# Layer 0's output projection: half of its contraction by Strassen's block products, two output tiles at a time

## The chip, the cores and the metric

The kernel runs on one core of a Trainium2 chip. The metric is the device time in microseconds (us) of one execution, as the median of several runs. The engines are named as in the profile: PE (TensorE matmul), PEld (its weight load), DVE (VectorE), ACT (ScalarE), POOL (GpSimd) and SP (SyncE, which only issues DMAs here).

## The reference, cut to what matters

One inference step of a two-layer decoder trunk over 576 tokens (512 prompt, 64 sample). Layer 0 is a short gated convolution, layer 1 an mLSTM block.

```python
def short_conv_mixer(h, buf, w_in, conv_w, w_out):
    b_gate, c_gate, xa, z = jnp.split(h @ w_in, 4, axis=-1)
    u = c_gate * xa
    conv, new_buf = causal_dwconv(u, buf, conv_w)
    y = b_gate * conv * jax.nn.silu(z)
    return y @ w_out, new_buf          # y: 576 x 2048, w_out: 2048 x 1024
...
x = x + out                            # residual, then layer 1
```

The change touches only `y @ w_out` of layer 0 and the addition to the residual.

## The kernel before, in words

Everything is kept transposed: a tile holds 128 features as partitions and the 576 tokens as columns. A product in float32 accuracy is made of three matmuls in a reduced format: each operand is split into a high part `hi` (an ACT cast) and a rest `lo` (a DVE subtraction), and `step` and `plain` issue weight-hi x data-hi, weight-hi x data-lo and weight-lo x data-hi. Each of these needs two matmuls, since 576 columns don't fit in one bank: `gemm` (L235) cuts them as 256 and 320 (`HALVES`), `plain` (L433) as 288 and 288 (`HT`).

Weights lie in HBM as chunks of 128 outputs x 1024 contraction rows, in the order in which they are used. A chunk is loaded by SP into one of four raw buffers (`wr`, 512 KB) and converted in halves of four 128x128 blocks: ACT cast `wh`, DVE subtraction `wl` (L215/L216 in `split_weights`, L264/L265 in `parts_of`), into four rotating buffers each.

Layer 0's input projections already use Strassen's scheme (in Winograd's form) in `block_pair`: two output tiles by two contraction tiles, the 576 columns cut in halves, seven products of 288 columns instead of eight. Its weight sums come from the blocks `a11, a12, a21, a22` of two raw chunks; in layer 0 (`layer0[0]` true) two of them are made by DMA: POOL issues accumulating loads (L312, L313), the others by DVE (L350, L354). Its data forms come from `forms(xa, xb)`: eight DVE operations (four of 288 columns in `mixed`, L271 to L274; three subtractions of 576 columns, L167; one of 288, L288) and four ACT operations, where a plain split of two tiles takes two DVE operations and two ACT casts. The seven products are issued by `product` (L345) into PSUM banks `p`; ACT copies some banks (L357, L362, L365, L375, L378), DVE adds the rest.

For each of 16 feature tiles f, layer 0 makes u, the convolution `cv` and the gate z, and multiplies them (L614 to L663). Block products for f+1's u and for f's z and b alternate on PE. The result is split at once into `ya` (hi, lo): L166, L167. Tiles of 576 columns come from one pool of 70 slots (`N_SLOT`), scratch of layer 0 from a second one with 7 slots (`X`).

Then comes the output projection, the loop over the 8 output tiles m:

```python
for m in range(KD):
    acc = gemm(64 + 2 * m, 2, ya)     # 2 chunks x 8 tiles x 3 x 2 = 96 matmuls
    x = T(name="x")
    load(out=x, in_=io["xT"][m])
    nc.vector.tensor_tensor(x, flat(acc), x, ALU.add)      # L678
```

followed by a store of x, its split for layer 1 (`h2`: L169, L170) and the sum of squares (L460 to L464). Layer 1 begins with `gemm(80, ...)` over `h2`.

The order of the instructions on each engine is not the order of the text: a planner gives each engine, when the program is built, the earliest instruction in the text whose operands and buffers it thinks ready. The queues then run in that fixed order, and an instruction that waits holds up those behind it on its engine; this holds for SP's and POOL's DMA issues too.

The functions that the change touches, and the part of the main function that calls them:

Of the kernel before, what the change touches and what calls it, by code (L numbers as in the profile page):

```python
# [12 lines left out]
ALU = mybir.AluOpType  # L13
# [6 lines left out]
KD = D // P  # L20
# [47 lines left out]
def trunk(tc, io):  # L68
    nc = tc.nc
    ctx = ExitStack()  # L70
    with ctx:
# [90 lines left out]
        def split(src, scale=None, n=NT):  # L162

            hi, lo = R(n, "hi"), R(n, "lo")
            if scale is None:
                nc.scalar.copy(hi, src)  # L166
                nc.vector.tensor_tensor(lo, src, hi.bitcast(F32), ALU.subtract)  # L167
            else:
                last_hi[:] = [nc.scalar.activation(hi, src, AF.Copy, scale=scale).ins]  # L169
                nc.vector.scalar_tensor_tensor(lo, src, scale, hi.bitcast(F32), ALU.mult, ALU.subtract)  # L170
            return hi, lo
# [151 lines left out]
            ahead_of[c1, c2] = groups, behind  # L323

        def block_pair(c1, c2, fs, xs, out1, out2, add, mid=None, then=None, pops=0, groups=None,
                       behind=()):

# [69 lines left out]
            if xs is None:  # L397
                tt(o22, p, m5, ALU.subtract)
# [26 lines left out]
        def plain(ba, bb, chunk, xs, start, w=()):  # L425

            w = w or weights(chunk)
            n = 4 * len(w)
            for k in range(n):
                (hi, lo), (xh, xl) = w[k // 4], xs[k]  # L430
                for i, (a, x) in enumerate(((hi, xh), (hi, xl), (lo, xh))):
                    for b, t in ((ba, 0), (bb, HT)):
                        nc.tensor.matmul(b, a[:, k % 4, :], x[:, t:t + HT], start=bool(start) and k == 0 and i == 0,  # L433
                                         stop=(k == n - 1 and i == 2), skip_group_check=True)
                if k % 2:
                    run()
                    if n == 8:
                        drip()

        def gemm_pair(c1, c2, fs, xs, out1, out2, mid=None, then=None, pops=0):  # L440


            if (c1, c2) not in ahead_of:
                block_weights(c1, c2)
            block_pair(c1, c2, fs, xs, out1, out2, False, mid, then, pops)
# [12 lines left out]
        def sumsq(ssq, x, first, eng=nc.vector):  # L458
            if first:
# [140 lines left out]
        nc.vector.tensor_tensor(rb2, rb, rb, ALU.mult)  # L600

        cpa = const.tile([P, NW, 2], F32, name="cpa")
        ya = []
        ext = None
        cx = raws[0:2]
        for f in range(NW):
# [54 lines left out]
            nc.scalar.activation(z, z, AF.Silu)  # L661
            nc.vector.tensor_tensor(cv, b_ if second else product(3), cv, ALU.mult)
            nc.vector.tensor_tensor(cv, cv, z, ALU.mult)  # L663
            ya.append(split(cv))
            if f % 4 == 3:
                store(out=io["exa_out"][f // 4], in_=ext)
        load_buffers("C", "states1", 2)
        layer0[0] = False
        store(out=io["cpa_out"], in_=cpa)

        x1s = dram.tile([KD, P, NT], F32, name="x1s")
        ssq = T(name="ssq")
        h2 = []
        for m in range(KD):
            acc = gemm(64 + 2 * m, 2, ya)
            x = T(name="x")
            load(out=x, in_=io["xT"][m])
            nc.vector.tensor_tensor(x, flat(acc), x, ALU.add)  # L678
# [945 lines left out]
def _arrays(a):  # L1624
# [6 lines left out]
    wts = np.concatenate([t.reshape(-1, P, KD, P) for t in (  # L1631
        ain, _chunks(f["a_w_out"][0]), bin_[:NW], _chunks(f["b_w_v"][0]), kq, bin_[NW:], _chunks(f["b_w_out"][0]))], 0)

    blk = [c for c in range(8, 64) if c % 4 < 2 or c // 4 in SECOND]
    wts[blk] = wts[blk][:, :, [0, 2, 4, 6, 1, 3, 5, 7]]
    cols = np.zeros((P, NCOL), np.float32)

# [81 lines left out]
```

## Time and profile before

| what | value |
|---|---|
| runs (3) | 1655.02, 1655.08 (median), 1656.1 us |
| span of the profiled execution | 1654.3 us (its time with what lies around the span isn't recorded apart) |
| PE busy | 1627.4 us, 98% of the span |
| DVE, ACT, POOL busy | 1125.8, 806.9, 148.8 us |
| granted TensorE clock, mean | 0.994 |

Layer 0's block products fill the span up to about 376 us, the output projection runs from there to about 489 us, layer 1 follows. A row of a window view gives, after the window's bounds and length, the busy time of PE, PEld, DVE, ACT and POOL with the instructions counted, then the granted clock (1.00 is full), the share of DMA and GB/s. A row of a timeline gives start, duration, engine, line, operation, output<-input, shape, and in brackets how long its engine sat idle before and what ended that. A group of instructions gives the count, the busy time, the mean ns of one, and the idle time before.

### The profile page before, as it was taken

To read this page: it belongs to the slowest core of one execution; us is meant where nothing else is said; L and a number is where in the kernel's file an instruction comes from. 1 tells how busy PE (TensorE), PEld (TensorE's weight loads), DVE (VectorE), ACT (ScalarE), POOL (GpSimd) and SP (SyncE) were. 2 spreads that over 40 slices of the span, in tenths; PEclk is the share of its full clock that TensorE was granted. 3 is DMA by queue.
4 is the path that set the end of the run, shared out by engine and by line. 5 is a ranking of instruction groups with operands and counts; after the bars stand their busy time and mean duration, and the time that the engine had idled before them with its cause. 6 is when DMAs were issued, how large, how long until landed. Compare 5 with 4: busy or idle time off the path is not lost. (4 is left out here: it accounts for less than half of the span.)

```text
span 1654.3 us, 31177 instructions
## 1 busy us (share of the span) xinstructions
PE 1627.4 (98%) x12029; PEld 1548.7 (94%) x12029; DVE 1125.8 (68%) x2124; ACT 806.9 (49%) x1622; POOL 148.8 (9%) x295
## 2 busy tenths in 40 slices
PE   9999999999999999999999999999999998999998
PEld 9999999999999999999899989899898787989997
DVE  7988898885337976555966456446458658688775
ACT  5566666653324553434645344344345456556431
POOL 1111111110001000000111010110101000000000
PEclk9999999999999999999999999999999899999999
DMA  6476666654332434535434554454556587998992
GB/s 219 111 174 167 175 168 159 175 136 148 120 120 91 149 121 128 172 119 159 156 103 151 156 177 162 142 188 140 173 190 241 186 280 262 336 341 296 359 342 103
DMA packets 121893, 301.61 MB, mean 182 GB/s; under 512 B 12656, under 2 KB 35056, under 8 KB 121744
## 3 DMA queue, kind: packets, MB, share of 16 engines
q1 hardware_dynamic: 98320, 267.61, 48.7%
q0 software_dynamic: 8064, 14.68, 5.8%
q10 hardware_dynamic: 15360, 17.32, 3.1%
q8 instruction: 94, 1.54, 0.4%
q14 instruction: 55, 0.45, 0.1%
HBM read 235.91 MB, written 63.66 MB: 181 GB/s over the span
## 5 line engine op out<-in xcount | busy, mean ns | idle before, releaser
L345 PE MATMUL p<-hi,wh 128*128 128x288 f32 x1540 | 454.4, 297 | 3.9 <-ACT p L357 1.9
L345 PE MATMUL p<-lo,wh 128*128 128x288 f32 x1540 | 452.6, 294 | 0.0
L345 PE MATMUL p<-hi,wl 128*128 128x288 f32 x1540 | 450.7, 295 | 0.2 <-DVE wl L265 0.2
L345 PEld LDWEIGHTS p<-hi,wh 128*128 128x128 f32 x1540 | 288.5, 188 | 12.7 <-DVE ws L350 4.1
L345 PEld LDWEIGHTS p<-lo,wh 128*128 128x128 f32 x1540 | 289.0, 188 | 0.0
L345 PEld LDWEIGHTS p<-hi,wl 128*128 128x128 f32 x1540 | 287.9, 188 | 0.4 <-DVE wl L265 0.4
L264 ACT CAST wh<-wr 128x512 fp32r<-128x512 f32 (+1 forms) x298 | 171.4, 578 | 215.4 <-PE p L345 123.5
L265 DVE TENSOR_TENSOR wl<-wr,wh 128x512 fp32r<-128x512 f32 (+1 forms) x298 | 185.0, 635 | 94.9 <-ACT wh L264 92.5
L235 PE MATMUL acc<-hi,wh 128*128 128x256 f32 (+1 forms) x1072 | 233.4, 298 | 1.8 <-ACT xm L711 1.0
L235 PE MATMUL acc<-lo,wh 128*128 128x256 f32 (+1 forms) x1072 | 231.9, 297 | 0.0
L235 PE MATMUL acc<-hi,wl 128*128 128x256 f32 (+1 forms) x1072 | 231.7, 297 | 0.0
L264 ACT CAST wh<-ws 128x512 fp32r<-128x512 f32 (+1 forms) x201 | 114.8, 573 | 203.8 <-PE p L345 129.6
L215 ACT CAST wh<-wr 128x512 fp32r<-128x512 f32 x170 | 104.7, 619 | 201.2 <-PE acc L235 148.1
L235 PEld LDWEIGHTS acc<-hi,wh 128*128 128x128 f32 x1072 | 180.4, 190 | 7.4 <-issue 1.6
L216 DVE TENSOR_TENSOR wl<-wr,wh 128x512 fp32r<-128x512 f32 x170 | 116.7, 689 | 98.7 <-ACT wh L215 88.6
L235 PEld LDWEIGHTS acc<-hi,wl 128*128 128x128 f32 x1072 | 179.9, 190 | 1.6 <-issue 1.3
L235 PEld LDWEIGHTS acc<-lo,wh 128*128 128x128 f32 x1072 | 179.9, 190 | 0.6 <-issue 0.2
L265 DVE TENSOR_TENSOR wl<-ws,wh 128x512 fp32r<-128x512 f32 (+1 forms) x201 | 125.5, 630 | 68.7 <-ACT wh L264 68.0
L1236 DVE SCALAR_TENSOR_TENSOR c<-c,cols,r 128x512 f32<-128x512 f32 x128 | 91.5, 743 | 27.0 <-PE r L1235 24.9
L433 PE MATMUL p<-hi,wh 128*128 128x288 f32 x496 | 109.2, 300 | 0.0
L433 PE MATMUL p<-hi,wl 128*128 128x288 f32 x496 | 107.3, 295 | 0.0
L433 PE MATMUL p<-lo,wh 128*128 128x288 f32 x496 | 107.0, 295 | 0.0
(388 smaller groups left out, 2619.1 us busy)
## 6 DMA issues: line engine op xcount, KB each, us to landing
wr<-wts SPq DMA_DIRECT2D x222, 512.0 KB, 3.6
c<-cs SPq DMA_DIRECT2D x112, 512.0 KB, 5.8
cs_out<-c SPq DMA_DIRECT2D x64, 512.0 KB, 7.5
ws<-wts SPq DMA_DIRECT2D x28, 256.0 KB, 4.5
ws<-wts POOLq DMA_DIRECT2D x28, 256.0 KB, 4.7
wr<-wts POOLq DMA_DIRECT2D x28, 256.0 KB, 4.1
x<-xcs SPq DMA_DIRECT2D x20, 288.0 KB, 4.8
x<-xT SPq DMA_DIRECT2D x16, 288.0 KB, 4.3
```

Source lines behind the costliest of these rows:

```text
L215: last_act[0] = nc.scalar.copy(hi, raw[:, 4 * i:4 * i + 4, :]).ins
L216: nc.vector.tensor_tensor(lo, raw[:, 4 * i:4 * i + 4, :], hi.bitcast(F32), ALU.subtract)
L235: nc.tensor.matmul(acc[:, o:o + j - i], a[:, k % 4, :], x[:, i:j], start=(first and k == 0 and p == 0), stop=(last and k == 7 and p == 2))
L264: last_act[0] = nc.scalar.copy(hi, src).ins
L265: nc.vector.tensor_tensor(lo, src, hi.bitcast(F32), ALU.subtract)
L345: nc.tensor.matmul(bank_, a[:, j, :], x, start=(start and n + j + i == 0), stop=(n == len(groups) - 1 and j == len(g) - 1 and i == 2), ski ...
L433: nc.tensor.matmul(b, a[:, k % 4, :], x[:, t:t + HT], start=bool(start) and k == 0 and i == 0, stop=(k == n - 1 and i == 2), skip_group_ch ...
L1236: ins = nc.vector.scalar_tensor_tensor(ct[:, j, :], ct[:, j, :], dec[:, o + j:o + j + 1], r, ALU.mult, ALU.add).ins
```

## The change

The contraction of 2048 is cut in two. Features 0 to 7 are multiplied as before, but by `plain` with equal halves; features 8 to 15 go through `block_pair`, for two output tiles (m, m+1) at a time, so four times. The tiles `ya[8:16]` are no longer split but kept as they are and made into `forms`: tiles 8 and 9 at f = 12, the other three pairs inside `gemm_first`, in the text behind the plain products of the first output pair. The first pair takes `gemm_first` (plain products first, then block products with the flag `add`), the other three take `gemm_pair` (block products first, then plain products into the same banks). With `onto`, the banks are added onto the residual rows, which are loaded ahead of the products. The store, the split and the sum of squares of two tiles follow each pair. Layer 0's scratch pool stays open until the projection is over, and the pool of the states opens there. On the host, the two chunks of each output tile change places and the blocks of one of them are reordered.

```diff
@@ block_pair(..., onto=False)
+            if onto:
+                tt(o12, o12, u, ALU.subtract)
+                plain(bx, bw, c1 + 1, xs, None)
+                tt(o11, bx, o11, ALU.add)
+                tt(o12, bw, o12, ALU.add)
+                tt(o22, o22, m5, ALU.subtract)
+                plain(by, bv, c2 + 1, xs, None)
+                tt(o21, by, o21, ALU.add)
+                tt(o22, bv, o22, ALU.add)
+                return
@@
-        def gemm_first(c1, c2, fs, xs, out1, out2, mid, then):
+        def gemm_first(c1, c2, fs, xs, out1, out2, mid, then, onto=False):
             mid = [go() for go in mid]
+            if onto:
+                block_weights(c1, c2)
             for c_, o in ((c1, out1), (c2, out2)):
                 ba, bb = block(), block()
                 plain(ba, bb, c_ + 1, xs, True)
-                nc.scalar.copy(o[:, 0:HT], ba)
-                nc.scalar.copy(o[:, HT:NT], bb)
-            work.extend([lambda: None, *mid])
-            block_pair(c1, c2, fs[0:4], None, out1, out2, True, then=then, pops=1)
+                for b, t in ((ba, 0), (bb, HT)):
+                    if onto:
+                        nc.vector.tensor_tensor(o[:, t:t + HT], b, o[:, t:t + HT], ALU.add)
+                    else:
+                        nc.scalar.copy(o[:, t:t + HT], b)
+            if onto:
+                for go in mid:
+                    go()
+            else:
+                work.extend([lambda: None, *mid])
+            block_pair(c1, c2, fs[0:4], None, out1, out2, True, then=then, pops=0 if onto else 1)
@@ layer 0, end of the loop over f
-            ya.append(split(cv))
+            ya.append(split(cv) if f < 8 else cv)
+            if f in (12,):
+                fy.append(forms(ya[8], ya[9]))
@@
-        load_buffers("C", "states1", 2)
-        layer0[0] = False
...
-        for m in range(KD):
-            acc = gemm(64 + 2 * m, 2, ya)
-            x = T(name="x")
-            load(out=x, in_=io["xT"][m])
-            nc.vector.tensor_tensor(x, flat(acc), x, ALU.add)
-            store(out=x1s[m], in_=x)
-            h2.append(split(x, col("norm1", m)))
-            sumsq(ssq, x, m == 0)
+        for m in range(0, KD, 2):
+            pair = [T(name="x") for _ in range(2)]
+            for i, x in enumerate(pair):
+                load(out=x, in_=io["xT"][m + i])
+            then = (68 + 2 * m, 70 + 2 * m) if m < KD - 2 else None
+            if m == 0:
+                more = [lambda j=j: lambda: fy.append(forms(ya[2 * j], ya[2 * j + 1])) for j in (5, 6, 7)]
+                gemm_first(64, 66, fy, ya[0:8], *pair, more, then, True)
+            else:
+                gemm_pair(64 + 2 * m, 66 + 2 * m, fy, ya[0:8], *pair, then=then, onto=True)
+            for i, x in enumerate(pair):
+                store(out=x1s[m + i], in_=x)
+                h2.append(split(x, col("norm1", m + i)))
+                sumsq(ssq, x, m + i == 0)
+        load_buffers("C", "states1", 2)
+        layer0[0] = False
@@ host
+    aout = _chunks(f["a_w_out"][0])[:, ::-1]
...
+    blk = [... as before ...] + list(range(64, 80, 2))
```

More of the change, by code (lines that the diff above doesn't have):

```diff
@@ L325, in block_pair @@
         def block_pair(c1, c2, fs, xs, out1, out2, add, mid=None, then=None, pops=0, groups=None,
-                       behind=()):
+                       behind=(), onto=False):
             if groups is None:
@@ L438, in plain, with gemm_pair @@
                         drip()
-        def gemm_pair(c1, c2, fs, xs, out1, out2, mid=None, then=None, pops=0):
+        def gemm_pair(c1, c2, fs, xs, out1, out2, mid=None, then=None, pops=0, onto=False):
             if (c1, c2) not in ahead_of:
                 block_weights(c1, c2)
-            block_pair(c1, c2, fs, xs, out1, out2, False, mid, then, pops)
-        def gemm_first(c1, c2, fs, xs, out1, out2, mid, then):
+            block_pair(c1, c2, fs, xs, out1, out2, False, mid, then, pops, onto=onto)
+        def gemm_first(c1, c2, fs, xs, out1, out2, mid, then, onto=False):
             mid = [go() for go in mid]
+            if onto:
+                block_weights(c1, c2)
             for c_, o in ((c1, out1), (c2, out2)):
@@ L602, in trunk @@
         cpa = const.tile([P, NW, 2], F32, name="cpa")
-        ya = []
+        ya, fy = [], []
         ext = None
@@ L1629, in _arrays @@
     bin_ = _chunks(f["b_w_in"][0])
+    aout = _chunks(f["a_w_out"][0])[:, ::-1]
     kq = np.stack([_chunks(f["b_w_k"][0]), _chunks(f["b_w_q"][0])], 1)
     wts = np.concatenate([t.reshape(-1, P, KD, P) for t in (
-        ain, _chunks(f["a_w_out"][0]), bin_[:NW], _chunks(f["b_w_v"][0]), kq, bin_[NW:], _chunks(f["b_w_out"][0]))], 0)
-    blk = [c for c in range(8, 64) if c % 4 < 2 or c // 4 in SECOND]
+        ain, aout, bin_[:NW], _chunks(f["b_w_v"][0]), kq, bin_[NW:], _chunks(f["b_w_out"][0]))], 0)
+    blk = [c for c in range(8, 64) if c % 4 < 2 or c // 4 in SECOND] + list(range(64, 80, 2))
     wts[blk] = wts[blk][:, :, [0, 2, 4, 6, 1, 3, 5, 7]]
```

## The prediction

> **What bounds the kernel now.** I read the page first, then a window view of the stretch in which the change lies and its neighbours.
>
> ```profile
> span 1654.3 us, 31177 instructions
> PE 1627.4 (98%) x12029; PEld 1548.7 (94%) x12029; DVE 1125.8 (68%) x2124; ACT 806.9 (49%) x1622; POOL 148.8 (9%) x295
> ...
> 300.00:340.00 40.00, 40.00 (x304) 40.00 (x304) 34.78 (x63) 25.16 (x53) 7.28 (x9) 1.00 0.68 171
> ...
> 360.00:390.00 30.00, 28.57 (x213) 28.10 (x213) 20.56 (x36) 14.24 (x28) 1.48 (x2) 1.00 0.45 135
> ...
> 404.00:482.00 78.00, 78.00 (x587) 78.00 (x587) 30.70 (x44) 23.56 (x37) 0.00 (x0) 1.00 0.40 132
> ```
>
> PE is the bound: busy 98% of the span, without a gap in the output projection (404 to 482) at clock 1.00, where DVE (30.7 of 78) and ACT (23.6) have much room. A matmul less there is time less. At the end of layer 0 it is different: DVE is busy 34.8 of 40 us before it, and across the transition (360 to 390) PE misses 1.43 us. Next, the timeline of DVE gives the rates and the waits:
>
> ```profile
> 118.61 0.45 DVE L398 TENSOR_TENSOR b<-pu,m 128x288 f32<-128x288 f32 x1
> ...
> 274.30 0.45 DVE L398 TENSOR_TENSOR b<-pu,m 128x288 f32<-128x288 f32 x1
> ...
> 365.79 0.69 DVE L354 TENSOR_TENSOR ws<-ws,wr 128x512 f32<-128x512 f32 x1 [1.53 <-DMA ws<-wts]
> ...
> 372.86 0.69 DVE L216 TENSOR_TENSOR wl<-wr,wh 128x512 fp32r<-128x512 f32 x1
> 373.46 0.75 DVE L167 TENSOR_TENSOR lo<-cv,hi 128x576 fp32r<-128x576 f32 x1
> 374.13 0.75 DVE L615 TENSOR_TENSOR u<-cx,cx 128x576 f32<-128x576 f32 x1
> ...
> 382.94 0.76 DVE L663 TENSOR_TENSOR cv<-cv,z 128x576 f32<-128x576 f32 x1
> ...
> 386.80 0.69 DVE L216 TENSOR_TENSOR wl<-wr,wh 128x512 fp32r<-128x512 f32 x1 [1.60 <-ACT wh L215]
> ...
> 389.61 0.76 DVE L678 TENSOR_TENSOR x<-acc,x 128x576 f32<-128x576 f32 x1 [2.12 <-PE acc L235]
> ...
> 479.21 0.76 DVE L678 TENSOR_TENSOR x<-acc,x 128x576 f32<-128x576 f32 x1 [2.08 <-PE acc L235]
> 480.81 0.82 DVE L170 SCALAR_TENSOR_TENSOR lo<-x,cols,hi 128x576 fp32r<-128x576 f32 x1 [0.25 <-ACT hi L169]
> ```
>
> The reader is to see three things. L678 ends each output tile: from 389.61 to 479.21 are seven tiles, so 12.80 us for 96 matmuls, 133.3 ns each. L398 of b ends a period of two block pairs (168 matmuls): seven periods from 118.61 to 274.30, 22.24 us each, 132.4 ns per matmul of 288 columns. And the last tile of layer 0 is ready only at 383.7 (L663), while u of that tile (L615) starts right behind the split that gives a slot back (L167).
>
> **Matmuls removed.** Before: 8 x 96 = 768 by 133.3 ns, 102.4 us. After, for each of four pairs: the plain half is 2 tiles x 8 x 3 x 2 = 96, the block half 7 products x 4 pairs of contraction tiles x 3 = 84, where plain needs 96. 4 x 180 = 720, all of 288 columns, by 132.4 ns: 95.3 us. The difference is 7.1 us: 6.4 from 48 matmuls and 0.7 from the equal halves. Nothing on PE hides this; it is the gain.
>
> The Trainium skill (TensorE: Matmul & The Clock Gate, Back-to-back issue gap) gives N/2.4 + 2.5 ns between warm matmuls, linear in the columns. By it 288 columns take 122.5 ns, equal halves gain nothing, and the saving would be an estimated 5.9 us; the row says 132.4, so the rule only fits within 8%, and I go by the row.
>
> **The transition, where the change adds work.** Ahead of the first block product stand two plain tiles, 96 x 132.4 ns = 12.7 us, which need only `ya[0:8]` and so start at the place of the old tile 0, to about 389.5. In that time three `forms` are to be made. How long one takes on DVE is seen in layer 1, together with what `gemm_first` costs there:
>
> ```profile
> 783.91 0.45 DVE L273 TENSOR_TENSOR fb<-x,x 128x288 f32<-128x288 f32 x1
> 784.28 0.45 DVE L274 TENSOR_TENSOR fb<-x,fa 128x288 f32<-128x288 f32 x1
> 784.64 0.69 DVE L216 TENSOR_TENSOR wl<-wr,wh 128x512 fp32r<-128x512 f32 x1
> 785.25 0.75 DVE L167 TENSOR_TENSOR lo<-fa,hi 128x576 fp32r<-128x576 f32 x1
> 785.92 0.75 DVE L167 TENSOR_TENSOR lo<-fb,hi 128x576 fp32r<-128x576 f32 x1
> 786.59 0.45 DVE L288 TENSOR_TENSOR hl<-x,hl 128x288 fp32r<-128x288 f32 x1
> 786.95 0.76 DVE L167 TENSOR_TENSOR lo<-x,hi 128x576 fp32r<-128x576 f32 x1
> ...
> L166 ACT CAST hi<-fa 128x576 fp32r<-128x576 f32 x14 | 9.4, 673 | 12.5 <-DVE fa L272 12.5
> ...
> PE p L345 <- ACT p L357: 1.9, 1, 1.9
> PE p L345 <- DVE hl L288: 0.7, 1, 0.7
> ...
> 800.00:815.00 15.00, 12.97 (x103) 11.45 (x102) 12.91 (x26) 10.21 (x23) 0.53 (x1) 1.00 0.38 116
> ```
>
> From start to start, 288 columns take 0.37 us, 576 take 0.67 and 512 take 0.60. A form is 5 x 0.37 + 3 x 0.67 = 3.9 us, three are 11.6. The ledger of DVE from 360 to 389.5 (29.5 us): 20.6 as before; less 1.3 (two splits), less 1.8 (seven halves of weights were converted there, L216 from 372.86 to 386.80; before the first block product only the four of chunks 65 and 67 are needed); plus 11.6; plus 2.4 (L354 and three L265 for the first products); plus 0.7 (two additions onto out1). That is 32.2 us. If u of the last tile is no longer held by a slot, its convolution (some 3 us from L615 on) moves ahead of 360 into DVE's gaps, and 29.1 are left. I expect that move: `ya[8:16]` as single tiles and one `forms` of 7 tiles hold about 68 of 70 slots at f = 15, some fewer than before. So PE would miss between 0 and 2.7 us, and the same function in layer 1 misses 2.03 (the window from 800 to 815, first for the last `hl`, then for the copy L357 that depends on the product so delayed). I take 2.0. ACT gets three casts of 0.67 us and a shorter copy per form, under 8 us in all, on top of 14.2 of 30, and is no bound.
>
> The wait of 1.43 us at 364 has another cause:
>
> ```profile
> 356.70 0.33 SPq L221 DMA_DIRECT2D wr<-wts  x1
> 357.07 0.42 SPq L311 DMA_DIRECT2D ws<-wts  x1
> ...
> SPq L221 <- DVE ws L350: 18.6, 2, 10.5
> ...
> 361.72 0.86 POOL L312 DMA_DIRECT2D ws<-wts  x1 [8.59 <-DMA ws<-wts]
> ```
>
> The load of chunk 64 waits on SP for a raw buffer until 356.70, and the load of a weight sum (L311) stands behind it; then POOL's accumulating load, then L354 at 365.79. In the new kernel two x loads and two block chunks come at this place and wait for the same buffer. I leave the 1.43 us in; its bounds are 0 and 1.43.
>
> **What moves or is added beside other work.** The forms of tiles 8 and 9 at f = 12: 3.9 us on DVE against 5 x 0.67 of splits that no longer come at f = 8 to 12; over one period of 22.2 us DVE (87% busy) would be full, and a weight conversion could be late by as much as about 1 us; I take 0, since conversions run two or three products ahead. Weights: 28 conversions of block weights take the place of 16 plain ones, 12 x 0.60 = 7.2 us more on DVE in 95 us, hidden under the 39% of that stretch. DMA: per pair a 256 KB load on SP and two accumulating ones on POOL more, at a DMA share of 0.40, with POOL idle there (0.00). The first plain weights (65, 67) come behind two block chunks on SP; before, the third and fourth loads were issued at 369.87 and 372.97 and
>
> ```profile
> 369.87 3.43 SPq L221 DMA_DIRECT2D wr<-wts  x2
> wr<-wts SPq DMA_DIRECT2D x222, 512.0 KB, 3.6
> ```
>
> land in 3.6 us: 65 is there at 373.5, converted by 375, needed at 376.6. That is covered by some 1.5 us; without that cover PE waits for the remainder. The additions onto x are six of 288 columns per pair instead of two of 576 (2.2 against 1.3 us start to start), under 11 us of other matmuls. The end: the last tile's additions, L169 and L170 end some 3 us after the last matmul (2 us before, from 479.2 to 481.6 at L170), and layer 1's first product needs that tile only for its last 6 of 48 matmuls, 5.6 us later; cost 0. The x loads now stand on SP ahead of their pair's weights, the stores behind the pair, as many as before; no engine waits for a store there.
>
> The three pairs of `gemm_pair` with `onto` have no row in this trace. Nearest is layer 1's `gemm_pair` with the same four raw buffers:
>
> ```profile
> L298 DVE TENSOR_TENSOR ws<-wr x39: 423/692/791, 552.3 to 1213.8; 128x512 f32<-128x512 f32 x24, 128x256 f32<-128x256 f32 x15
> ...
> 650.00:700.00 50.00, 50.00 (x384) 49.32 (x383) 29.92 (x53) 23.11 (x44) 3.62 (x8) 1.00 0.44 135
> ```
>
> The window has no idle time on PE: I take 0. Upper end: each waits once like f = 15 for its accumulated sum, 3 x 1.43 = 4.3 us. They have the plain half (12.7 us) as cover for a chain that took 8.7 us (357.07 to 365.79), so 0 is nearer. The first row shows when the states' pool is first written, at 552 us: that it now opens some 100 us later than before costs 0.
>
> **Sum.** -7.1 + 2.0 = -5.1 us. The span 1654.3 becomes 1649.2; the median of the runs, 1655.08, lies 0.8 above the span, so 1650.0.
>
> **Rivals.**
> A: nothing waits, and the 1.43 us go too, because the planner puts the sum's load ahead of the chunk on SP. For it speaks the ledger's lower end (29.1), against it that both `forms` and the last gate need DVE and ACT in turn. -8.5: 1646.6.
> B: the change doesn't deliver: the saving is handed back in waits, 32.2 us of ledger (2.7), hand-overs with ACT (1), and one wait per later half of the pairs (1 to 2). -7.1 + 5.5 = -1.6: 1653.5, no measurable change. DVE's 87% ahead of the transition speaks for it, the free 60% behind it against.
> C, slower: the planner keeps the forms in the text's order, behind the plain products' additions. Then DVE starts them at 389.5: 0.7 for the last additions, 11.6 for the forms, less the last 0.67, plus 0.67 for an ACT cast; only three quarters of the first two products (18 matmuls, 2.4 us) run meanwhile. PE misses 9.9 us. After 2.7 us without work in 4, the trace shows a lower clock:
>
> ```profile
> 1378.00:1382.00 4.00, 1.29 (x8) 1.06 (x8) 3.67 (x6) 3.71 (x12) 0.00 (x0) 0.94 0.54 148
> 1382.00:1386.00 4.00, 3.71 (x21) 3.31 (x20) 4.00 (x7) 2.23 (x5) 0.29 (x1) 0.64 0.71 249
> ```
>
> 0.36 of 4 us, 1.4 us more. -7.1 + 9.9 + 1.4 = +4.2: 1659.3. It is slower by 0.2% once the waits pass 10.4 us. Against it: L216 of chunk 64 (372.86) runs ahead of L615, which is earlier in the text, so DVE's order isn't the text's. The Trainium skill (TensorE: Matmul & The Clock Gate, Part 1) says an idle window of about 3.4 us halves the clock until about 3.4 us of work have passed; by that rule C would cost an estimated 1.7 instead of 1.4. The trace agrees: 1.00 after waits of 1.4 and 2.0 us, 0.64 after 2.7 in 4.
>
> **How the numbers follow.** The likeliest: 0.48. A 0.14, B 0.25, C 0.13. Measurement of this kernel tells 0.2%, 3.3 us. Faster (likeliest and A) 0.62, same (B) 0.25, slower (C) 0.13. The likeliest's own range is 1648 to 1652 (0 to 4 us of waits in the transition). The whole range reaches to A, 1646.5, and over B to 1655.5 (the three pairs waiting 4.3 and the transition 2.7, rounded up); C is left out.
>
> **What would show it.** Matmuls at L345 and L433 in the place of L235 between 376 and 482, and layer 1 starting 5 us earlier; PE idle behind `hl` or L357 near 389 of about 2 us (right), over 5 (B or C); the window of the later pairs with PE full; the forms' L271 of the last pairs before 389. Wrong it would be if PE waits for `wh` of the later pairs, or if the planner's new order opens gaps far behind, in layer 1.

## The result and the profile after

The changed kernel takes 1665.65 us (median of 4 runs, 1661.38 to 1666.48), the kernel before 1655.59 beside it; ratio 1.0053, interval 1.0039 to 1.0067. It is slower by more than the 0.2% that this kernel's measurement can tell, where 1650.0 had been forecast. The profiled execution is one of 1666.03 us.

The page after, and the window view of the stretch around the change (columns as before), first the kernel before over the whole stretch, then the changed one:

```profile
span 1664.2 us, 31238 instructions
PE 1626.0 (98%) x11981; PEld 1545.6 (93%) x11981; DVE 1150.2 (69%) x2188; ACT 823.9 (50%) x1658; POOL 156.4 (9%) x303
```
```profile
340.00:410.00 70.00, 68.57 (x514) 68.10 (x514) 46.56 (x77) 33.35 (x64) 3.80 (x5) 1.00 0.48 139
```
```profile
300.00:345.00 45.00, 44.40 (x335) 44.17 (x335) 41.50 (x77) 29.03 (x61) 8.56 (x11) 1.00 0.67 166
360.00:375.00 15.00, 13.53 (x101) 13.10 (x100) 9.06 (x17) 7.26 (x16) 2.33 (x3) 1.00 0.51 137
375.00:390.00 15.00, 14.30 (x105) 13.75 (x105) 12.16 (x23) 7.93 (x17) 0.87 (x1) 1.00 0.64 187
390.00:400.00 10.00, 5.36 (x34) 4.57 (x33) 10.00 (x22) 3.44 (x6) 0.86 (x1) 0.92 0.45 114
400.00:410.00 10.00, 7.95 (x36) 7.64 (x37) 4.72 (x9) 4.90 (x10) 0.86 (x1) 0.57 0.22 35
340.00:410.00 70.00, 61.15 (x423) 59.06 (x422) 53.93 (x101) 35.90 (x72) 6.84 (x9) 0.93 0.52 135
412.00:490.00 78.00, 78.00 (x589) 78.00 (x588) 46.81 (x79) 36.92 (x65) 3.48 (x4) 1.00 0.57 168
```

The 48 matmuls are gone (12029 to 11981) and the later pairs run without a gap (412 to 490). The loss lies in the transition: from 340 to 410 PE is idle for 8.85 us instead of 1.43, with the clock at 0.92 and 0.57 where it was 1.00, and gets 91 matmuls less done (423 against 514), 12.1 us at 133 ns. Another 0.6 us is missing between 300 and 345, where the first form is made. (The projection of the kernel before ends at about 479 us, with the last L678 of the prediction's view, not at the 489 us given further above.)

To compare kernels I cut the span at four milestones: the first normalisation (`ms` from `sums`), the last store of `x1s`, the first sums of layer 1's gate (`gs`), and the last `ms`. The rows, of the kernel before and then of the changed one (min/median/max in ns, then first and last start):

```profile
L477 DVE TENSOR_SCALAR ms<-sums x6: 145/153/160, 34.8 to 1645.6; 96x3 f32<-96x3 f32 x4, 80x4 f32<-80x4 f32 x1, 128x2 f32<-128x2 f32 x1
L679 SPq DMA_DIRECT2D x1s<-x x8: 326/327/327, 390.4 to 480.0; - x8
L1027 PE MATMUL gs<-gacc,cst x4: 379/431/483, 1258.4 to 1260.0; 128*64 128x256 f32 x2, 128*64 128x320 f32 x2
```
```profile
L496 DVE TENSOR_SCALAR ms<-sums x6: 146/153/159, 36.3 to 1655.2; 96x3 f32<-96x3 f32 x4, 80x4 f32<-80x4 f32 x1, 128x2 f32<-128x2 f32 x1
L704 SPq DMA_DIRECT2D x1s<-x x8: 326/326/327, 412.7 to 487.9; - x8
L1054 PE MATMUL gs<-gacc,cst x4: 378/430/483, 1265.5 to 1267.1; 128*64 128x256 f32 x2, 128*64 128x320 f32 x2
```

Stretch A, to the last store of x1s, is layer 0 with the projection: 445.2 us before, 451.6 after. The middle is 778.4 and 777.6; stretch C, from `gs` to the last `ms`, is 387.2 and 389.7. So of 9.9 us of span, 6.4 are layer 0 with the projection, 2.5 the late part and 1.5 the start; the middle gives 0.8 back. The same milestones of all profiled executions follow. Each ratio is taken against runs of the kernel before in the same batch, whose medians were 1655.59 to 1656.24 us. One of the 12 runs of e7 was a slow one of 3953.74 us and is left out of its median and ratio.

| kernel | A | middle | C | median us | ratio to before, interval |
|---|---|---|---|---|---|
| before | 445.2 | 778.4 | 387.2 | 1655.59 | |
| before again (e8) | 444.8 | 778.9 | 386.0 | one run, 1655.3 | |
| halves alone (e7) | 447.0 | 779.1 | 388.0 | 1655.99 | 0.9999, 0.9988 to 1.0010 |
| changed | 451.6 | 777.6 | 389.7 | 1665.65 | 1.0053, 1.0039 to 1.0067 |
| changed again (e10) | 450.7 | 777.4 | 387.9 | one run, 1662.12 | |
| no forms (e1) | 441.9 | 777.7 | 392.1 | 1654.27 | 0.9996, 0.9987 to 1.0006 |
| no sums (e2) | 446.3 | 777.6 | 389.4 | 1658.1 | 1.0012, 1.0002 to 1.0021 |
| order on SP (e3) | 447.0 | 777.6 | 391.6 | 1660.63 | 1.0029, 1.0013 to 1.0045 |
| kept warm (e4) | 449.8 | 777.8 | 389.8 | 1664.19 | 1.0055, 1.0040 to 1.0070 |
| two pairs first (e5) | 441.7 | 777.8 | 394.1 | 1655.94 | 0.9998, 0.9987 to 1.0009 |
| two pairs first again (e11) | 443.5 | 778.6 | 391.2 | one run, 1659.38 | |
| order of need (e6) | 445.2 | 777.5 | 386.9 | 1657.42 | 1.0007, 0.9997 to 1.0018 |
| both (e9) | 441.4 | 778.5 | 386.9 | 1652.78 | 0.9981, 0.9972 to 0.9990 |

**What PE waits for.** The waits of PE in the changed kernel from 340 to 410 (us in total, times, longest), and its timeline at the first block product:

```profile
PE p L345 <- ACT hl L287: 5.1, 2, 2.6
PE p L345 <- DVE hl L288: 1.6, 2, 1.2
PE p L345 <- ACT wh L264: 1.2, 1, 1.2
```
```profile
396.71 0.40 PE L345 MATMUL p<-hl,wh 128*128 128x288 f32 x1 [2.59 <-ACT hl L287]
398.35 0.60 PE L345 MATMUL p<-hl,wh 128*128 128x288 f32 x1 [1.24 <-DVE hl L288]
401.73 0.61 PE L345 MATMUL p<-hl,wh 128*128 128x288 f32 x1 [2.54 <-ACT hl L287]
402.65 0.61 PE L345 MATMUL p<-hl,wh 128*128 128x288 f32 x1 [0.32 <-DVE hl L288]
```

The first product needs `hl` of all four forms; it gets the third and the fourth late. **Why they are late** stands on DVE, POOL and SP (the queue of SP as SPq; three cuts of one timeline):

```profile
367.32 0.69 DVE L354 TENSOR_TENSOR ws<-ws,wr 128x512 f32<-128x512 f32 x1 [4.66 <-DMA ws<-wts]
...
368.67 0.74 DVE L634 TENSOR_TENSOR u<-cx,cx 128x576 f32<-128x576 f32 x1
...
378.41 0.44 DVE L271 TENSOR_TENSOR fa<-cv 128x288 f32<-128x288 f32 x1
...
382.66 0.69 DVE L354 TENSOR_TENSOR ws<-ws,wr 128x512 f32<-128x512 f32 x1 [2.84 <-DMA ws<-wts]
...
388.79 0.75 DVE L682 TENSOR_TENSOR cv<-cv,z 128x576 f32<-128x576 f32 x1
...
402.15 0.45 DVE L288 TENSOR_TENSOR hl<-cv,hl 128x288 fp32r<-128x288 f32 x1
```
```profile
363.26 0.86 POOL L312 DMA_DIRECT2D ws<-wts  x1 [7.31 <-DVE wl L265]
...
369.48 0.58 POOL L637 COPY cpa<-u 128x2 f32<-128x2 f32 x1 [3.38 <-DVE u L634]
375.74 0.87 POOL L312 DMA_DIRECT2D ws<-wts  x1 [5.68 <-ACT wh L264]
```
```profile
357.79 1.13 SPq L311 DMA_DIRECT2D ws<-wts  x1
...
370.09 0.34 SPq L688 DMA_DIRECT2D cpa_out<-cpa  x1
372.02 0.34 SPq L687 DMA_DIRECT2D exa_out<-ext  x1
372.48 0.36 SPq L311 DMA_DIRECT2D ws<-wts  x1
```

Read it in the order of time. SP issues the load of a weight sum (L311) at 357.79, behind block chunks that waited for a raw buffer. POOL adds the second half at 363.26, and DVE stands at L354 for 4.66 us until that has landed; before, it stood there 1.53 us (365.79). The order on DVE is fixed, and now L398, L400 and u of the last tile (L634) are behind L354, where L398 and L400 had been ahead of it (362.57 in the kernel before). So u comes at 368.67, POOL's copy from u at 369.48, and SP, which stands at the store of that copy (L688), goes on only at 370.09. The load of the second weight sum stands behind that store and the next one (L687, which waits for a copy that DVE makes of the same u) and goes out at 372.48. DVE then waits for it too, 2.84 us, with the forms and the last gate behind: L682 ends the last feature tile at 388.79, where L663 did it at 382.94. So one late load holds up the next, across three queues; e3 below tests this reading.

**The clock.** Short windows of the changed kernel:

```profile
398.00:400.00 2.00, 0.84 (x2) 0.50 (x2) 2.00 (x5) 0.00 (x0) 0.00 (x0) 0.60 0.81 312
404.00:408.00 4.00, 4.00 (x18) 4.00 (x18) 1.38 (x2) 1.18 (x3) 0.00 (x0) 0.50 0.16 29
408.00:410.00 2.00, 2.00 (x15) 2.00 (x14) 0.35 (x1) 0.92 (x2) 0.00 (x0) 0.84 0.00 0
```

From 404 to 408 PE is never idle and yet only 18 matmuls are counted in 4 us; in the timeline they start 0.24 us apart, where it was 0.13 before. From 402.65, where the last of the waits ends, to 408.6 that loses some 2.5 us. The Trainium skill (TensorE: Matmul & The Clock Gate, Part 1) has a clock of half speed after an idle window and full speed only after about 3.4 us of sustained work. The trace agrees on the half speed (0.50); full speed came back 5.9 us after the last wait, later than that figure.

### The profile page after: what moved, and what is told of

It reads as the page before. It is cut to its first block, busy times and chain, and to the rows that moved or that the text cites. A ratio compares the mean times of both kernels' runs of the same rounds, so it can differ in the third digit from the quotient of the medians.

```text
span 1664.2 us, 31238 instructions
## 1 busy us (share of the span) xinstructions
PE 1626.0 (98%) x11981; PEld 1545.6 (93%) x11981; DVE 1150.2 (69%) x2188; ACT 823.9 (50%) x1658; POOL 156.4 (9%) x303
## 5 line engine op out<-in xcount | busy, mean ns | idle before, releaser
L345 PE MATMUL p<-hi,wh 128*128 128x288 f32 x1636 | 484.0, 298 | 3.5 <-ACT p L357 1.4
L345 PE MATMUL p<-lo,wh 128*128 128x288 f32 x1636 | 482.0, 295 | 0.0
L345 PE MATMUL p<-hi,wl 128*128 128x288 f32 x1636 | 478.8, 296 | 0.6 <-DVE wl L265 0.6
L345 PEld LDWEIGHTS p<-hi,wh 128*128 128x128 f32 x1636 | 307.9, 189 | 12.7 <-DVE ws L350 4.1
L265 DVE TENSOR_TENSOR wl<-ws,wh 128x512 fp32r<-128x512 f32 (+1 forms) x213 | 133.3, 631 | 73.3 <-ACT wh L264 73.1
L235 PE MATMUL acc<-hi,wh 128*128 128x256 f32 (+1 forms) x816 | 178.2, 299 | 2.1 <-ACT xm L738 1.0
L235 PE MATMUL acc<-lo,wh 128*128 128x256 f32 (+1 forms) x816 | 177.2, 297 | 0.0
L235 PE MATMUL acc<-hi,wl 128*128 128x256 f32 (+1 forms) x816 | 176.9, 297 | 0.0
L235 PEld LDWEIGHTS acc<-hi,wh 128*128 128x128 f32 x816 | 136.9, 190 | 7.7 <-issue 1.6
L235 PEld LDWEIGHTS acc<-hi,wl 128*128 128x128 f32 x816 | 136.8, 190 | 1.7 <-issue 1.3
L235 PEld LDWEIGHTS acc<-lo,wh 128*128 128x128 f32 x816 | 136.8, 190 | 0.5 <-issue 0.2
L443 PE MATMUL p<-hi,wh 128*128 128x288 f32 x592 | 129.7, 299 | 0.0
L443 PE MATMUL p<-hi,wl 128*128 128x288 f32 x592 | 128.1, 295 | 0.0
L443 PE MATMUL p<-lo,wh 128*128 128x288 f32 x592 | 127.8, 295 | 0.0
```

The costliest lines, as they stand in the source:

```text
L235: nc.tensor.matmul(acc[:, o:o + j - i], a[:, k % 4, :], x[:, i:j], start=(first and k == 0 and p == 0), stop=(last and k == 7 and p == 2))
L345: nc.tensor.matmul(bank_, a[:, j, :], x, start=(start and n + j + i == 0), stop=(n == len(groups) - 1 and j == len(g) - 1 and i == 2), ski ...
```

## The experiments

Two explanations of the stalls were set against each other, and against a third place of the loss: V, the volume of the forms on DVE in the short time that the first two plain tiles cover; Q, the queues, where work stands behind the late weight sums; L, the late part of the program.

**e1: no forms.** The three forms in `gemm_first` are left out; the block products use the form of tiles 8 and 9 for all pairs, as many matmuls as before.

```diff
-more = [lambda j=j: lambda: fy.append(forms(ya[2 * j], ya[2 * j + 1])) for j in (5, 6, 7)]
+more = [lambda j=j: lambda: fy.append(fy[0]) for j in (5, 6, 7)]
```

> Leaves out the three forms made in gemm_first (tiles 10 to 15): the block products take the forms of tiles 8 and 9 in their place. Matmuls, weights and DMAs stay. Theory V (volume: DVE has more to do at the transition than two plain tiles of 12.7 us cover) and theory Q (queues: DVE stands twice behind late weight sums, 4.7 and 2.8 us, and so the last gate and the forms are late) both expect the PE idle time of 6.7 us from 394 to 404 and the lower clock behind it (some 2.7 us) gone: about 9.4 us less than the changed kernel, 1656. Rival L (the loss is spread: a later start, and a plan of layer 1 that came out worse) expects no more than 5 us less, 1661.

1654.27 us, ratio 0.9996 (0.9987 to 1.0006), and stretch A is 9.7 us shorter than in the changed kernel. The window in which that one had 5.36 of 10:

```profile
390.00:400.00 10.00, 10.00 (x77) 10.00 (x77) 5.81 (x11) 4.00 (x8) 1.57 (x2) 1.00 0.48 116
```

So the idle time of that window goes with the forms, and the clock stays at 1.00. V and Q had both expected 1656, and L 1661, so the main loss isn't in the late part. But A is only 3.3 us under the kernel before, less than the 6.4 us of matmuls taken out: other waits (2.8 us in all from 340 to 410, where the kernel before has 1.43) are left without these forms.

**e2: no sums.** The accumulating loads of `s1` for the chunk pairs 62/63 and 64/66 are left out, so two weight sums miss one term.

```diff
-add_load(out=s1, in_=io["wts"][c2][:, 4:8, :], accum_op=ALU.add)
+if c1 not in (62, 64):
+    add_load(out=s1, in_=io["wts"][c2][:, 4:8, :], accum_op=ALU.add)
```

> Leaves out the two accumulating loads on POOL that complete the weight sums s1 of the chunk pairs 62/63 and 64/66 (those sums stay half); everything else is as in the changed kernel. Theory Q: DVE is no longer held at 363 and 380, the last gate comes 3 to 6 us earlier, the forms end about 7 us earlier (near 396), PE misses 0 to 3 us instead of 7 and the clock stays: 7 to 9 us less, 1657 to 1659. Theory V: DVE is full anyhow, at most the 1.4 us at 364 and 1 to 2 us more: 1662 to 1664. Rival L: 1.4 us less, 1664.

**e3: order on SP.** The load of the first sum goes ahead of the block chunks 64 and 66, the load of the second one ahead of the two stores. Nothing is left out.

```diff
-latest[0] = load(out=r, in_=io["wts"][c_]).ins
+with tc.issue_after(sum_load[0]) if c1 == 64 else nullcontext():
+    latest[0] = load(out=r, in_=io["wts"][c_]).ins
...
-load(out=s1, in_=io["wts"][c2][:, 0:4, :])
+sum_load[0] = load(out=s1, in_=io["wts"][c2][:, 0:4, :]).ins
...
 block_weights(c1, c2)                     # in gemm_first
+with tc.issue_after(sum_load[0]):
+    store(out=io["exa_out"][NW // 4 - 1], in_=ext)
+    store(out=io["cpa_out"], in_=cpa)
```

> Nothing left out, only SP's order: the load for the sum of 62/63 is issued ahead of chunks 64 and 66, and the load for the sum of 64/66 ahead of the two stores cpa_out and exa_out. POOL still copies the last cpa ahead of the second accumulating load. Theory Q: the wait at 364 goes (1.4 us), DVE's 2.8 us at 380 goes, the last gate comes 3 us earlier: 5 to 8 us less than the changed kernel, 1658 to 1661. Theory V: 1 to 3 us less, 1663 to 1665. Rival L: 0 to 1.4 us less.

e2 takes 1658.1 us (1.0012, 1.0002 to 1.0021), e3 1660.63 (1.0029, 1.0013 to 1.0045); stretch A comes down by 5.3 and 4.6 us (4.4 and 3.7 against the repeat of the changed kernel, e10). Both times lie where Q expected them. The windows of e3:

```profile
360.00:375.00 15.00, 14.78 (x108) 14.13 (x107) 11.83 (x23) 8.09 (x17) 1.97 (x3) 1.00 0.66 164
375.00:390.00 15.00, 15.00 (x115) 15.00 (x114) 14.43 (x29) 8.76 (x16) 0.86 (x1) 1.00 0.56 161
390.00:398.00 8.00, 3.26 (x14) 2.25 (x13) 7.29 (x15) 3.74 (x8) 0.86 (x1) 0.84 0.34 99
```

Q is right for the first part: with the sums on time PE misses 0.2 us from 360 to 390, and DVE does 26.3 us of work there instead of 21.2 (9.06 + 12.16). V is right for the rest: the plain tiles now end earlier, DVE isn't done with the forms, and PE still misses 4.7 of the 8 us that follow. Neither explanation is enough by itself.

**e4: kept warm.** 70 extra matmuls of 256 columns, whose result nobody uses, stand behind the plain tiles, so that PE works while it waits.

```diff
 if onto:
+    with tc.issue_after(last_plain[0]):
+        warm_up(70)
     for go in mid:
         go()
```

> Adds 70 matmuls on a constant tile (256 columns, bf16) behind the two plain tiles, ahead of the first block product: PE works some 7.6 us where it waited. The forms come no earlier. If the half clock from 398 to 408.5 costs what its rows say (22 matmuls of 0.24 instead of 0.132 us and some ahead), the time falls by 2.4 to 2.7 us, to 1663.3; if the lower clock only covers a wait that is there anyhow, it stays at 1666; if the filler delays the block products, it rises by up to 3 us.

1664.19 us, ratio 1.0055 (1.0040 to 1.0070), not to be told from the changed kernel's 1.0053; A is 1.8 us shorter than in that one's first profile and 0.9 than in its second.

```profile
400.00:410.00 10.00, 9.69 (x76) 9.29 (x75) 7.25 (x14) 5.55 (x11) 0.86 (x1) 1.00 0.34 75
```

The clock stays at 1.00, where the changed kernel had 0.57 in this window, but the forms come when DVE has them. The time lies between the two values expected, so what the lower clock costs by itself isn't settled: A gains 0.9 to 1.8 us, and A of one kernel differs between two executions by 0.4 to 1.8 us. The clock is a consequence and not the cause.

**e5: two pairs first.** The plain products of the first two output pairs stand ahead of the first block product, 25.6 us of cover instead of 12.8. SP issues the weight sums as early as in e3, here by holding back chunk 65; the block weights of the first pair stand behind its plain products in the text.

```diff
-gemm_first(64, 66, fy, ya[0:8], *pair, more, then, True)
+gemm_two([(64, 66, *pair[0:2]), (68, 70, *pair[2:4])], fy, ya[0:8], more, [(68, 70), (72, 74)])
```

`gemm_two` runs `plain` and the additions for both pairs, then the forms, then two `block_pair`.

> The plain products of the first two output pairs (four tiles, 25.4 us) come ahead of the first block product, in place of one pair (12.7 us), and SP issues the weight sums as in the kernel with the new SP order. Matmuls and forms are those of the changed kernel. Theory V+Q (DVE's work for the forms ends some 7 us after the cover of one pair, even with SP's order mended): with twice the cover PE misses nothing at the first block product and the clock stays 1.00; layer 1 begins 5.5 to 7 us earlier than in the kernel before (last store of x1s at 473 to 475 us instead of 480.0), so 5 us less than the run with the new SP order. If the cover isn't what lacks, the idle time comes back ahead of another block product: last store at 480 or later. Rival L (late part of the run 2 to 5 us longer whatever the transition does): the whole time is then 1651 to 1653, else 1648 to 1650.

```profile
375.00:412.00 37.00, 37.00 (x281) 37.00 (x280) 29.97 (x59) 17.95 (x33) 2.60 (x3) 1.00 0.51 153
412.00:430.00 18.00, 15.69 (x114) 14.89 (x112) 12.96 (x24) 10.36 (x22) 2.62 (x3) 1.00 0.73 182
```

PE is full where the changed kernel stalled, and A is 441.7: 9.9 us less than there and 3.5 less than before. The last store of `x1s` comes at 476.6, though, not at the 473 to 475 expected. A wait of 2.3 us comes at 412 to 430, 2.1 of it for the cast of the second pair's block weights. The median, 1655.94 (0.9998, 0.9987 to 1.0009), shows none of these 3.5 us; the profile, of an execution 3.4 us above the median, has them lost again in stretch C (394.1). Once the queues are in order, what is left of the stalls goes with more cover, as V has it.

**e6: order of need.** The three forms are made in stages: first all `hl` (first product), then `fa` with its split, then `xb`, then `fb`; one pair first, and the order on SP of e3.

```diff
-for go in mid:
-    go()
+staged = [go() for go in mid]      # hl | fa, split | split(xb) | fb, split
+for stage in range(4):
+    for s_ in staged:
+        s_[stage]()
```

> Only one pair of plain products first, SP's order mended, and the three forms written in the order in which the block products need their parts: all three hl, then the first mixed tiles, then the splits of the second tiles, then the second mixed tiles. The same operations on DVE. If what counts is when the last hl is there (volume V in the order in which it is worked off), the first product no longer waits; DVE's work then spreads under products 1 to 5, which wait 0 to 3 us in all; the clock stays 1.00: 4 to 6 us less than the run with the new SP order, 1655. If the volume alone counts, PE waits as long, only behind later products: 1660.

1657.42 us, 1.0007 (0.9997 to 1.0018); A is 445.2. PE's two longest waits between 375 and 412:

```profile
377.94 0.53 PE L476 MATMUL blk<-hi,wh 128*128 128x288 f32 x2 [1.25 <-ACT wh L215]
404.29 0.40 PE L378 MATMUL p<-hi,wh 128*128 128x288 f32 x1 [1.75 <-ACT wh L264]
```

The first product waits for no `hl` any more. What is late instead are casts of weights: at 404 the block weights that stand behind the forms on ACT and DVE, and at 377.94 the first plain weights (chunk 65). The work that doesn't fit has moved to the next consumer, and the time lies between the two that were expected (1655 and 1660).

**e7: halves alone.** The kernel before, with `plain` in equal halves for all 8 tiles and no Strassen.

```diff
-acc = gemm(64 + 2 * m, 2, ya)
-nc.vector.tensor_tensor(x, flat(acc), x, ALU.add)
+ba, bb = block(), block()
+plain(ba, bb, 64 + 2 * m, ya[0:8], True)
+plain(ba, bb, 65 + 2 * m, ya[8:16], None)
+for b, t in ((ba, 0), (bb, HT)):
+    nc.vector.tensor_tensor(x[:, t:t + HT], b, x[:, t:t + HT], ALU.add)
```

> The kernel before with one part of the change alone: each output tile by plain with two halves of 288 columns (no block products, no forms), added onto the residual loaded ahead. The prediction's term of 0.7 us for the equal halves: last store of x1s at 479.3 instead of 480.0. The plan of the late part (from 1300 us) comes out a little different from before, as in all runs of the change. Rival L by plan: the late part is 2 to 4 us longer here too, 1657; if the late part is as before: 1654.5.

1655.99 us, 0.9999 (0.9988 to 1.0010). The stores of `x1s` and two windows of e7, and the same windows of the kernel before:

```profile
L682 SPq DMA_DIRECT2D x1s<-x x8: 326/326/327, 391.8 to 481.4; - x8
```
```profile
360.00:366.00 6.00, 5.26 (x40) 5.03 (x39) 1.99 (x5) 0.85 (x3) 0.86 (x1) 1.00 0.63 153
366.00:372.00 6.00, 5.28 (x26) 5.04 (x27) 5.27 (x9) 4.13 (x9) 0.00 (x0) 0.72 0.17 40
```
```profile
360.00:366.00 6.00, 5.28 (x40) 5.04 (x39) 2.01 (x5) 0.86 (x3) 0.86 (x1) 1.00 0.57 150
366.00:372.00 6.00, 5.29 (x38) 5.06 (x39) 5.27 (x9) 5.10 (x12) 0.00 (x0) 1.00 0.18 38
```

Seven tiles in 89.6 us are 12.80 a tile, as with 256 and 320 columns: equal halves gain nothing, and the last store is at 481.4 instead of the 479.3 expected. The windows show why it is even later than before: the idle time around the weight sum at 364 is the same in both kernels (1.46 and 1.43 us from 360 to 372), but in e7 the clock falls to 0.72 behind it and 12 matmuls less get done in the same busy time, 1.6 us.

**e8: before again.** The kernel before, unchanged, to see how far milestones repeat.

> The kernel before once more, unchanged, as a control for the trace: how much its start (sums of layer 0 at 34.8 us) and its late part (1258.4, the gate sums, to 1645.6, the last sums: 387.2 us) vary between executions on their own. If they vary by 2 us or more, the later start and the longer late part of the other runs say nothing; if by less than 0.5, they are due to the plan.

1655.3 us; A 444.8 against 445.2, C 386.0 against 387.2. The difference in C, 1.2 us, lies between the two limits that had been set (0.5 and 2), so by itself it decides nothing.

**e9: both.** e5 and e6 in one, with the second pair's block weights in the text ahead of the forms.

```diff
...
+block_weights(*pairs[1][0:2])
+staged = [go() for go in mid]
+for stage in range(5):
+    for s_ in staged:
+        s_[stage]()
```

> All edits that helped, in one kernel: the plain products of the first two output pairs first (25 us of cover), the forms in stages in the order of need, the chunks and stores behind the load of the sum on SP, and the block weights of the second pair in the text ahead of the forms. Theory (volume and queues together): nothing is left for PE to wait for between 360 and 490 but the 1 to 2 us that stay at 412 to 430 where a weight cast is late; the last store of x1s comes at 475.5 to 477 of the span (before 480.0, two plain pairs first alone 476.6), 3 to 4.5 us earlier than before. If the late part (gate sums to last sums of squares) costs what it did in the kernel before (387 us), the median is 1651 to 1653, ratio 0.997 to 0.9985; if every form of the kernel with block products pays 2 to 4 us there, as the profiles so far have it, it is 1654 to 1656, ratio 0.999 to 1.0005. Rival (the stalls are not the forms' but the chip's, whatever the order): the last store at 480 or later and the median at 1657 or above.

1652.78 us, ratio 0.9981 (0.9972 to 0.9990): 3.2 us faster than the kernel before in that batch (1656.01), and the only version of the change that beats it. Two windows and the last store:

```profile
375.00:412.00 37.00, 37.00 (x280) 37.00 (x279) 31.32 (x61) 18.39 (x34) 1.72 (x2) 1.00 0.55 164
412.00:430.00 18.00, 16.59 (x122) 16.02 (x121) 13.88 (x24) 11.02 (x21) 2.62 (x3) 1.00 0.65 163
```
```profile
L758 SPq DMA_DIRECT2D x1s<-x x8: 326/326/327, 411.0 to 476.5; - x8
```

A is 441.4, 3.8 us under before, with full cover and 1.4 us of waits left at 412 to 430. C is 386.9, as in the kernel before. This is the outcome of the theory of volume and queues together, with a late part that costs what it did. Against e5, A is 0.3 us shorter and C 7.2 (2.1 and 4.3 against e11): most of what e9 gains on e5 lies in the late part, which its edits don't touch.

**e10: the changed kernel again**, for its milestones.

> The changed kernel once more, unchanged, for its milestones. If the 1.6 us at its start and the 2.5 us in its late part belong to that one execution, this one has its first sums of layer 0 at 34.4 to 35.2 of the span and a late part of 386 to 388, and a span near 1660; if they belong to the kernel, the start is again at 36 and the late part at 389.5 or more, with a span of 1663 to 1665. The transition is the same either way: from the first sums to the last store of x1s 451 to 452 us (before 445.2, and 444.8 in the repeat of before).

Span 1660.3, as expected if the execution made the difference: A 450.7, C 387.9, first normalisation at 35.4. (The start is 0.2 us beyond the range given for that, A 0.3 below.) So the loss in A stands (5.9 us over e8), while 0.9 of the 1.5 us at the start and 1.8 of the 2.5 in C belonged to the first execution.

**e11: two pairs first again.**

> The kernel with the two plain pairs first once more, unchanged, for its late part. In its first profile that part took 394.1 us, 7 more than before, while its median is 4 us below that profile. If the late part is a matter of the execution, it takes 387 to 391 here and the span is 1651 to 1655; if the order that the planner made for it there is slower, it takes 393 to 395 again, with a span of 1657.

Span 1657.6, C 391.2, A 443.5. C came down by 2.9 us and A went up by 1.8. C lies between the two expectations; neither is borne out.

## Why the prediction was wrong, point by point

**The matmuls: right in the main term.** 48 fewer, 6.4 us. The 0.7 us for equal halves were wrong: e7 gains nothing per tile. The 132.4 ns had come from block products and the 133.3 from plain ones, and I read the difference as one of columns. The Trainium skill (TensorE: Matmul & The Clock Gate, Back-to-back issue gap), which the prediction set aside, has a time linear in the columns, for an isolated matmul. That equal halves gain nothing agrees with it; the estimate of 122.5 ns for 288 columns doesn't (133.3 in this stream, with as many weight loads as matmuls).

**The transition: the step that failed.** The term was 2.0 us, and it measured 7.4 us of idle PE beyond the 1.43 of before, plus some 2.5 at the lower clock. The ledger's volume was near: it asked for 29.1 to 32.2 us of DVE work up to 389.5, and DVE did 34.2 us from 360 to the end of the forms at 403.3, some conversions for later products among them. The step that failed is the comparison with the 29.5 us at hand, as if DVE could work through all of them. DVE worked 21.2 of the 30 us up to 390. It stood 7.5 us (4.66 + 2.84) at the two sums of L354, and the forms ended at about 403 instead of 390. The row of L354 with its 1.53 us was in the prediction, and I left 1.43 us in as a price for PE only. What stands behind it on DVE, and through u and POOL's copy on SP, was not followed. e3 shows what that omission was worth: 3.7 to 4.6 us of A, and 5.0 of the median. What remains after e3 is the second fault: even without those waits 12.7 us of cover are too short, by the 4.7 us of idle that e3 still has. The prediction's upper end for the whole transition was 2.7.

**"I expect that move."** It happened only in part: u of the last tile came 5.5 us earlier (368.67 against 374.13), not ahead of 360, since it was placed behind L354. The last gate came 5.9 us later, not earlier.

**The wait at 364.** It stayed, as left in: PE's 1.47 us from 360 to 375 in place of 1.43.

**The analog in layer 1** (2.03 us) misled. There DVE makes the weight sums itself, so no accumulating load stands ahead of the forms; it waits for the tiles that the forms are made of, 1.5 us at 782.75 and 0.3 us at 783.53. I took a price from a place with the same code and other neighbours.

**The rivals.** C came nearest in size (9.9 us of idle PE and 1.4 of clock; 7.4 and some 2.5 were measured), but by luck, since its mechanism was another: that the text's order holds the forms back behind the plain products' additions. The first of the three forms started at 378.41, some 15 us before the plain products ended. The other two started at 391.90 and 398.88, behind additions (390.50) that take only 0.8 us; DVE was busy without a gap from 383.27 to 400 and simply late. B's 5.5 us of handed-back waits were too few, and the waits measured lay in the transition, not in the later pairs.

**Beside other work.** The form at f = 12, taken as 0 with an upper end of about 1, costs 0.6 us (44.40 of 45). The three later pairs cost 0, as forecast:

```profile
457.61:481.52 23.91, 23.91 (x182) 23.91 (x181) 13.41 (x23) 10.76 (x19) 0.00 (x0) 1.00 0.47 157
```

This is one pair of output tiles, from store to store: 96 x 133.3 + 84 x 132.4 ns = 23.92 us, without a gap. DVE has more to do there than the prediction added (46.8 of 78 us from 412 to 490, 30.7 before), but it isn't what PE waits for.

**The sum in A.** -6.4 for the matmuls, +7.4 idle, +2.5 clock, +0.6 at f = 12 make +4.1, against +6.4 measured (5.9 in the repeat). By the count of matmuls it closes better: 91 too few from 340 to 410 and 7 from 300 to 345 are 13.0 us, less 6.4 is 6.6. So 2 us or so are matmuls that took longer. Missing records don't explain them, since the counts of the whole span differ by just the 48 taken out. Most of them start behind a wait: the matmuls at 396.71, 398.35, 401.73 and 402.65 take 0.4 to 0.6 us each until the next one starts or they end, and with the one that follows at 398.75 that is some 1.6 us more than at 0.13 us each.

**The late part, open in part.** The median is 10 us up and A only about 6. The prediction named new gaps far behind, in layer 1, as something that would make it wrong. The middle stretch has none, but C has one. At 1541.81 PE waits 4.20 us for DVE in the changed kernel, 3.60 in its repeat and 4.89 in e3; neither execution of the kernel before has this wait, nor has e9. It begins on ACT, which stands for a load (`kss`) with a copy behind it; DVE waits 4.79 us for the copy, and PE for DVE. First the changed kernel, then the kernel before at the same place:

```profile
1534.93 0.72 ACT L1163 ACTIVATE ld<-ld,cols 128x512 f32<-128x512 f32 x1 [8.32 <-DMA ld<-kss]
...
1541.81 0.52 PE L1316 MATMUL cp<-vh,hi 128*128 128x256 f32 x1 [4.20 <-DVE ld L1431]
```
```profile
1524.40 0.72 ACT L1136 ACTIVATE ld<-ld,cols 128x512 f32<-128x512 f32 x1 [5.30 <-DMA ld<-kss]
```

Why the load comes later isn't shown. C, taken as unchanged, is 386.0 to 394.1 us in 13 executions, with the same 2618 or 2619 matmuls in each. PE is idle in C for 11.9 and 11.3 us in the two executions of the kernel before and for 14.5 and 13.8 in those of the changed kernel, so the excess of the latter is idle time. In e5 it is mostly the clock: the same matmuls keep PE busy for 380.8 us (375.3 before), and the time at half clock, summed from the granted clock in windows of 2 us, is 27.3 us against 17.1. One kernel differs from itself in C by 1.2 (before), 1.8 (changed) and 2.9 us (two pairs first). Block products in layer 0 don't fix C: e6 and e9 have 386.9. The other versions with them lie 0.7 to 6.9 us above the kernel before, and no run told an order made by the planner from the chance of one execution.

## What to carry to other kernels

A ledger of an engine's work against the time at hand holds only if the engine can work all that time: list first the waits that stand in its fixed order, with the row of each, and follow what is queued behind them on that engine, and behind its consumers on the others. When products are put ahead as cover for work that makes operands, size the cover by that work plus those waits, make first what is needed first, and look which consumer is next in line when it moves. A price taken from the same function elsewhere in the program is worth only as much as its neighbours there are alike.

## What the hardware showed that was not expected

A short wait can cost a second time. Behind nearly equal waits of PE (1.43 and 1.46 us in 12) the granted clock stayed at 1.00 in the kernel before and fell to 0.72 in e7, with 26 instead of 38 matmuls in the same 5.3 us of busy time. The lower clock of e7 lasted some 3.4 us (0.92, 0.50 and 0.72 in the three windows of 2 us from 366). Seven profiled executions have 1.1 to 2.1 us of waits between 364 and 372; in the other six the clock stayed at 1.00. The prediction took waits of that length to leave the clock alone, from one execution. The Trainium skill (TensorE: Matmul & The Clock Gate, Part 1) calls the window that watches PE's activity free-running; that fits a drop which depends on when the wait comes, though the idle time here was far below that page's 3.4 us.

How long a load took to land didn't go by its size. From POOL's issue of an accumulating load of 256 KB to the add that waits for it passed 4.1 and 6.9 us in the changed kernel (363.26 to 367.32, 375.74 to 382.66). The page of the kernel before has medians from issue to landing of 4.7 us for these loads, 4.5 us for the plain loads of 256 KB into the same tiles and 3.6 us for the plain loads of 512 KB. So it isn't shown that accumulating makes a load slower.
